# One transformer block on one core: a first tile in plain float32, two fewer dot products on TensorE, and a rewritten tail

## The chip, the core and the metric

The kernel runs on one core of one Trainium2 chip. The time is the device time of one execution in microseconds (us); lower is better. Before the change it is 1208.03 us, the median of three runs (1205.26 to 1211.31 us). The execution that was profiled took 1210.78 us, of which the profile's span covers 1209.1 us. Time zero in every table is the span's start.

## The reference

What is computed is one block over 512 tokens of width 1024, all in float32, with feature-major activations (a tile holds 128 features of all 512 tokens):

```python
mod = einsum('bd,de->be', silu(c), w_ada) + b_ada
shift1, scale1, gate1, shift2, scale2, gate2 = split(mod, 6)
hmix = modulate(rmsnorm(x, g_norm1), shift1, scale1)      # h*(1+scale)+shift
proj = einsum('bsd,de->bse', hmix, w_in)                  # 16 stick-breaking heads, 4 retention heads, gates
...
x = x + gate1 * einsum(merged, w_out)
hffn = modulate(rmsnorm(x, g_norm2), shift2, scale2)
a, u = split(einsum(hffn, w_ffn_in), 2)
x = x + gate2 * einsum(silu(a) * u, w_ffn_out)
return rmsnorm(x, g_final)
```

Three places matter here. The **opening** makes shift1 and scale1 (each of their 1024 values is a dot product of a column of w_ada with silu(c)), the modulated rmsnorm, and the projections of the first retention head. The **last product** is the one with w_ffn_out, and the **tail** adds it to the residual, takes the mean of squares over the features for each token, and writes the scaled result.

## The kernel before

TensorE multiplies float32r operands. To keep float32 accuracy nearly every matrix product is made of three: each operand is split into a high part (a copy rounded to float32r, made by ScalarE) and a low part (the remainder, made by VectorE), and the three products high*high, low*high and high*low are summed in PSUM.

**The opening** (lines 435 to 546) is written in a fixed order for TensorE, VectorE and ScalarE (`manual_schedule`): each engine runs its instructions as the program lists them. The eight steps kt = 0 to 7 go over the eight feature tiles. Step kt multiplies the modulated tile `hs[kt]` with 768 weight columns: 256 each of the first retention head's q, k and v. `qk_products` makes the q and k part (four products of 512 columns, or eight of 256), `v_products` the v part (four of 256). For each tile n the other engines prepare:

- `dot(n, half)` on VectorE (line 384): the dot products for the shift (half 0) or the gain (half 1), a 128x1024 multiplication with accumulation. `PE_SHIFT` lists the tiles whose shift is made by TensorE instead, by `dot_pe(n)` (line 393): eight float32 products with one column. Before, the list is 0, 1 and 4.
- `mod_shift` and `mod_gain` on ScalarE (lines 400, 405): the two 128x1 columns.
- `h_t` on VectorE (line 422): x times gain times the row scale, into `ts[n]`; `h_hi` on ScalarE (line 428): adds the shift and rounds to the high part; `h_lo` on VectorE (line 431): the low part.
- `w_hi` on ScalarE (line 411) and `w_lo` on VectorE (line 415): the parts of the weights.

The rows of w_ada and the weights come by DMA, issued in order by SP, into 8 buffers (`sraw`, two per tile) and 3 buffers (`raw`, one per step). `keep_busy(n)` (line 453) issues n products whose result nobody reads.

**Between** the opening and the last product the instructions are ordered by the framework's scheduler, not by hand. The remaining dot products with w_ada (line 254, on VectorE, fed by DMA into two buffers called `araw`) are spread through this part by it, up to about 180 us.

**The tail** (lines 1327 to 1374) is ordered by hand again. Eight output tiles d each get a product (`gemm`), a residual (VectorE, line 924: x1 = product*gate + x1), squares (ScalarE, line 1345), and a sum of squares over tiles (VectorE, line 1201, `add_square`). Tiles 0 to 2 are done whole; tiles 3 to 7 (`LAST`) in token halves h0 (0 to 255) and h1 (256 to 511). A product with a matrix of ones sums over the partitions (`mm(s0, ones, ...)`, in float32); `rsqrt_rows` (lines 320 to 324: two ScalarE and three VectorE instructions) makes the row scale; `final_norm` (line 1133, VectorE) scales a tile's half and sends it to memory, on ScalarE's queue for odd tiles of h1 and on SP's for the rest.

Of the kernel before, what the change touches and what calls it, by code (L numbers as in the profile page):

```python
# [14 lines left out]
AF = mybir.ActivationFunctionType  # L15
# [19 lines left out]
C_RQ, C_RK, C_RV, C_RG, C_BR = 3072, 4096, 5120, 7168, 9216  # L35


PE_SHIFT = (0, 1, 4)


FF_CHUNKS = ((0, 1), (1, 2), (3, 2), (5, 2), (7, 2), (9, 2))
# [72 lines left out]
def kernel(  # L114
# [44 lines left out]
    def f(ap):  # L159
        return ap.bitcast(F32)  # L160
# [274 lines left out]
    with tc.manual_schedule(engines={nc.vector.engine, nc.scalar.engine, nc.tensor.engine}):  # L435

        nc.scalar.preload_act_table_set("natural_log_exp_and_others")
        c = sm[:, SM_C : SM_C + KT]
        nc.scalar.activation(ccol, c, AF.Exp, scale=-1.0)
        nc.vector.tensor_scalar(ccol, ccol, 1.0, None, op0=ALU.add)  # L440
        nc.vector.reciprocal(ccol, ccol)
        nc.vector.tensor_mul(ccol, ccol, c)
        cb = [psz(), psz()]
        for k in range(KT):
            mm(cb[k // 4][:, (k % 4) * P : (k % 4 + 1) * P], ccol[:, k : k + 1].to_broadcast([P, P]),
               ident, k % 4 == 0, k % 4 == 3)
# [6 lines left out]
        def keep_busy(n):  # L453


            for _ in range(n):
                mm(busy, negones, negones[:, 0:1].to_broadcast([P, S]), True, True)

        keep_busy(6)

        sq = {}
        for j in range(KT):
            sq[j] = tmp()
            if j == 3:
                nc.vector.tensor_mul(sq[j], xts[j], xts[j])
            else:
                nc.scalar.activation(sq[j], xts[j], AF.Square)
            if j == 4:
                nc.vector.tensor_copy(cact[:, 0:S], cb[0])
            elif j == 6:  # L470
                nc.scalar.activation(cact[:, S:], cb[1], AF.Copy)
            if 0 < j < 6:
                nc.vector.tensor_add(sq[0], sq[0], sq[j])
# [24 lines left out]
        def qk_products(w, act, hv, start=False, stop=False):  # L498
            for i in range(4):
                mm(qk_ps[i][:, hv], w[:, i * P : (i + 1) * P], act[:, hv], start, stop)  # L500

        def v_products(act, w, blocks, start=False, stop=False):
            for b in blocks:
                o = v_ps[b // 2][:, (b % 2) * 256 : (b % 2) * 256 + 256]
                mm(o, act[:, b * P : (b + 1) * P], w[:, 512:768],
                   start and b % 2 == 0, stop and b % 2 == 1)

        for kt in range(KT):
            if kt == 3:
                nc.vector.tensor_copy(negtri, con[:, P : 2 * P])  # L510
            nx = kt + 1
            if nx + 1 < KT:
                raws[nx + 1] = ada_load(nx + 1)
                wts[nx + 1] = start_weight(nx + 1)
            if nx < KT and nx not in PE_SHIFT:
                dot(nx, 0)
            h_lo(kt)
            _, hi, lo = wts[kt]
            ah, al = hs[kt][:, 0, :], hs[kt][:, 1, :]
            z = kt == KT - 1  # L520
            if kt == 0:
                for n, hv in enumerate(HALVES):
                    qk_products(hi, ah, hv, n == 0)
                    v_products(ah, hi, (2 * n, 2 * n + 1), True)
                if 1 in PE_SHIFT:
                    dot_pe(1)
                qk_products(lo, ah, ALL)
                v_products(ah, lo, range(4))
            else:
                qk_products(hi, ah, ALL)  # L530
                qk_products(lo, ah, ALL)
                if nx + 1 in PE_SHIFT:
                    dot_pe(nx + 1)
                v_products(ah, hi, range(4))
                v_products(ah, lo, range(4))
            qk_products(hi, al, ALL, False, z)
            v_products(al, hi, range(4), False, z)
            if nx < KT:
                dot(nx, 1)
                mod_shift(nx)  # L540
                mod_gain(nx)
                w_lo(nx)
                h_t(nx)
                h_hi(nx)
            if nx + 1 < KT:
                w_hi(nx + 1)
# [789 lines left out]
    with tc.manual_schedule(engines={nc.vector.engine, nc.scalar.engine, nc.tensor.engine}):  # L1336
        banks = {d: ps() if d < 7 else psa() for d in LAST}

        def out_half(d, hv):
            gemm(banks[d][:, hv], wts[d], acts, t0=hv.start, t1=hv.stop)  # L1340

        def out_square(d, hv):
            residual(d, banks[d], 40, hv)
            sq = tmp()[:, 0:256]
            nc.scalar.activation(sq, x1[d][:, hv], AF.Square)  # L1345
            return sq

        for d in LAST:
# [3 lines left out]
        r = tmp()  # L1352
        out_half(3, h1)
        mm(s0, ones, acc[:, h0], True, True)
        rsqrt_rows(s0, r[:, h0])
        add_square(out_square(3, h1), h1)
        for d in LAST[1:4]:
            out_half(d, h1)
        for d in LAST[1:3]:
            add_square(out_square(d, h1), h1)  # L1360
        for d in range(3):
            final_norm(d, h0, r[:, h0])
        add_square(out_square(6, h1), h1)
        out_half(7, h1)
        mm(s1, ones, acc[:, h1], True, False)
        for d in range(3, 5):
            final_norm(d, h0, r[:, h0])
        sq = out_square(7, h1)
        mm(s1, ones, sq, False, True)
        for d in range(5, 8):  # L1370
            final_norm(d, h0, r[:, h0])
# [68 lines left out]
```

## Time and profile before

| what | number |
|---|---|
| median of three runs | 1208.03 us (1205.26 to 1211.31) |
| profiled execution | 1210.78 us, span 1209.1 us |
| TensorE busy (products) | 1182.2 us, 98% of the span |
| VectorE busy | 830.5 us, 69% |
| ScalarE busy | 555.0 us, 46% |
| opening, to the end of step kt = 7 | up to 58.46 us |
| tail, from the first half product to the end | 1178.95 to 1209.1 us |

PE stands for TensorE's products and PEld for its loads of the stationary operand, DVE for VectorE, ACT for ScalarE, POOL for GpSimd and SPq for the DMA issues of SyncE. A row of the timeline has the start, the busy time, the engine, the line, the operation, the tiles (written <- read), the shapes, the number of instructions merged into the row, and in brackets how long the engine sat idle before it and whom it waited for. L226 is the helper through which every product goes, so products are told apart by their tiles. A row of the windows has the busy time of each engine in the stretch, the clock that TensorE was granted (1.00 is full) and the DMA engines' share. A float32 product shows as two records, a float32r product as one.

### The profile page before, as it was taken

How to read it: one execution, taken by the hardware profiler on the slowest of the kernel's cores; microseconds unless marked ns; L12 is line 12 of the kernel's file. 1: busy time of each engine (PE TensorE's matmuls, PEld its weight loads, DVE VectorE, ACT ScalarE, POOL GpSimd, SP SyncE). 2: the span in 40 equal slices, each digit the busy share in tenths (PEclk: the TensorE clock that was granted, in tenths of full speed). 3: DMA queues.
4: the chain of work that ended last, by engine and by line, in shares of the span. 5: the costliest groups of instructions: out<-in, count | busy, mean ns of one | idle time of the engine just before them, and what ended most of it. 6: DMA issues, size and time to landing. Idle time of an engine off the chain costs nothing.

```text
span 1209.1 us, 17051 instructions
## 1 busy us (share of the span) xinstructions
PE 1182.2 (98%) x6739; PEld 1038.7 (86%) x6739; DVE 830.5 (69%) x1274; ACT 555.0 (46%) x823; POOL 31.4 (3%) x60
## 2 busy tenths in 40 slices
PE   8999999999999999999999999999999999999995
PEld 7887777888888888898989888889999999999985
DVE  6888886545555534377878888756988776677656
ACT  5443223332332322377677777345844444454332
POOL 0010000000000000000000000000100000000000
PEclk8999999999999999999999999999999999999998
DMA  9746772231243155535353635643446653565322
GB/s 358 247 131 226 233 252 71 87 105 53 87 122 87 55 149 147 147 92 126 101 136 97 161 82 160 232 122 96 100 137 174 184 161 106 149 185 142 104 71 70
DMA packets 53136, 167.72 MB, mean 139 GB/s; under 512 B 6592, under 2 KB 8768, under 8 KB 53056
## 3 DMA queue, kind: packets, MB, share of 16 engines
q1 hardware_dynamic: 49168, 154.04, 41.6%
q0 software_dynamic: 3312, 12.06, 5.4%
q8 instruction: 53, 0.87, 0.3%
q10 hardware_dynamic: 576, 0.52, 0.1%
q14 instruction: 27, 0.22, 0.1%
HBM read 135.67 MB, written 4.19 MB: 116 GB/s over the span
## 4 chain that ended last, share of the span: by engine, by line
PE 85%; DVE 6%; DMA 4%; ACT 2%; issue 2%; POOL 0%; SPq 0%; DVEq 0%; POOLq 0%; ACTq 0%
PE ps L226 61%; PE z L226 21%; DMA araw<-wada 3%; PE av L226 3%; DVE araw L254 1%; DVE o L1133 0%; DMA o<-xT 0%; DMA h<-h 0%; DVE o L924 0%; ACT h L1208 0%; DVE wlo L207 0%; DVE t L1201 0%; ACT t L1345 0%; DMA t<-t 0%; ACT t L625 0%
## 5 line engine op out<-in xcount | busy, mean ns | idle before, releaser
L226 PE MATMUL ps<-h,whi 128*128 128x512 f32 (+1 forms) x1419 | 418.8, 377 | 0.1
L226 PEld LDWEIGHTS ps<-h,whi 128*128 128x128 f32 x1419 | 258.3, 189 | 44.7 <-ACT h L428 0.7
L205 ACT ACTIVATE whi<-raw 128x1024 fp32r<-128x1024 f32 (+1 forms) x138 | 144.3, 1046 | 283.3 <-PE ps L226 248.4
L226 PE MATMUL ps<-h,wlo 128*128 128x512 f32 (+1 forms) x708 | 264.4, 377 | 0.0
L207 DVE TENSOR_TENSOR wlo<-raw,whi 128x1024 fp32r<-128x1024 f32 (+1 forms) x138 | 166.3, 1206 | 93.5 <-ACT whi L205 56.5
L226 PEld LDWEIGHTS ps<-h,wlo 128*128 128x128 f32 x708 | 133.6, 189 | 23.3
L226 PE MATMUL ps<-s,whi 128*128 128x512 f32 x480 | 149.3, 392 | 1.9 <-DVE v L207 1.9
L226 PE MATMUL ps<-whi,h 128*128 128x256 f32 (+1 forms) x480 | 115.0, 326 | 1.5 <-DVE t L679 1.5
L226 PE MATMUL z<-q,whi 128*128 128x256 f32 x504 | 108.6, 285 | 0.0
L226 PEld LDWEIGHTS ps<-s,whi 128*128 128x128 f32 x480 | 90.1, 190 | 20.5 <-DVE v L207 2.4
L226 PE MATMUL ps<-s,wlo 128*128 128x512 f32 x240 | 94.1, 392 | 0.0
L207 DVE TENSOR_TENSOR s<-t,s 128x512 fp32r<-128x512 f32 (+1 forms) x122 | 77.0, 651 | 24.0 <-ACT s L205 23.7
L226 PEld LDWEIGHTS ps<-whi,h 128*128 128x128 f32 x480 | 82.4, 190 | 10.1 <-DVE t L679 2.3
L205 ACT ACTIVATE s<-t 128x512 fp32r<-128x512 f32 (+1 forms) x122 | 70.8, 598 | 38.4 <-DVE t L789 22.8
L226 PEld LDWEIGHTS z<-q,whi 128*128 128x128 f32 x504 | 86.3, 194 | 1.5
L226 PE MATMUL ps<-wlo,h 128*128 128x256 f32 (+1 forms) x240 | 78.1, 325 | 0.0
L924 DVE SCALAR_TENSOR_TENSOR o<-ps,mod,o 128x512 f32<-128x512 f32 (+1 forms) x63 | 42.4, 680 | 34.7 <-PE ps L226 34.6
L226 PEld LDWEIGHTS ps<-s,wlo 128*128 128x128 f32 x240 | 45.4, 189 | 9.7
L226 PEld LDWEIGHTS ps<-wlo,h 128*128 128x128 f32 x240 | 45.6, 190 | 4.0
L226 PE MATMUL ps<-q,whi 128*128 128x256 f32 (+1 forms) x224 | 48.9, 313 | 0.0
L226 PE MATMUL z<-qp,whi 128*128 128x256 f32 x168 | 47.3, 283 | 0.9 <-DVE t L1314 0.9
L226 PE MATMUL z<-q,wlo 128*128 128x256 f32 x168 | 47.9, 285 | 0.0
(259 smaller groups left out, 1843.2 us busy)
## 6 DMA issues: line engine op xcount, KB each, us to landing
raw<-wp SPq DMA_DIRECT2D x163, 512.0 KB, 3.7
araw<-wada SPq DMA_DIRECT2D x32, 512.0 KB, 4.4
araw<-wp SPq DMA_DIRECT2D x22, 512.0 KB, 5.0
sraw<-wada SPq DMA_DIRECT2D x16, 512.0 KB, 7.8
q<-qp SPq DMA_DIRECT2D x32, 256.0 KB, 3.7
o<-xT SPq DMA_DIRECT2D x16, 256.0 KB, 4.0
q<-qp SPq DMA_DIRECT2D x32, 128.0 KB, 3.3
s<-raw POOLq DMA_DIRECT2D x8, 512.0 KB, 7.4
```

What stands on the lines that cost most here:

```text
L205: nc.scalar.activation(dst_hi, src, AF.Copy, scale=scale)
L207: (eng or nc.vector).tensor_sub(dst_lo, src, f(dst_hi))
L226: nc.tensor.matmul(o, lhs, rhs, start=start, stop=stop, skip_group_check=True)
L254: nc.vector.scalar_tensor_tensor(raw, raw, 1.0, cact, op0=ALU.mult, op1=ALU.mult, accum_out=col)
L924: nc.vector.scalar_tensor_tensor(x1[d][:, hv], o[:, hv], mod[:, gcol + d : gcol + d + 1], x1[d][:, hv], op0=ALU.mult, op1=ALU.add,)
```

## The change

In the opening, `PE_SHIFT` becomes (0,): the shifts of tiles 1 and 4 are made by VectorE. Step kt = 0 no longer works with parts: ScalarE adds the shift in place to `ts[0]`, and TensorE multiplies the float32 tile with the float32 weights as loaded. The high part of `hs[0]`, which later stages read, is made at step 5 and the low part at step 7. In the tail, the order of residuals, squares, additions and scalings is written anew, one sum over the partitions is moved between the products of tile 4, four products of `keep_busy` are put before the last sum, and tile 7's first half is scaled last.

```diff
-PE_SHIFT = (0, 1, 4)
+PE_SHIFT = (0,)
@@ opening
         h_t(0, HALVES[1])
-        w_hi(0)
         mod_shift(0)
         for hv in HALVES:
-            h_hi(0, hv)
-        w_lo(0)
+            nc.scalar.activation(ts[0][:, hv], ts[0][:, hv], AF.Identity, bias=mods[0, 0])
+        hs.append(pair("h"))
         w_hi(1)
...
-            h_lo(kt)
-            _, hi, lo = wts[kt]
+            if kt:
+                h_lo(kt)
+            raw, hi, lo = wts[kt]
...
             if kt == 0:
                 for n, hv in enumerate(HALVES):
-                    qk_products(hi, ah, hv, n == 0)
-                    v_products(ah, hi, (2 * n, 2 * n + 1), True)
-                if 1 in PE_SHIFT:
-                    dot_pe(1)
-                qk_products(lo, ah, ALL)
-                v_products(ah, lo, range(4))
+                    qk_products(raw, ts[0], hv, n == 0)
+                    v_products(ts[0], raw, (2 * n, 2 * n + 1), True)
             else:
...
-            qk_products(hi, al, ALL, False, z)
-            v_products(al, hi, range(4), False, z)
+                qk_products(hi, al, ALL, False, z)
+                v_products(al, hi, range(4), False, z)
+            if kt == 5:
+                nc.scalar.activation(hs[0][:, 0, :], ts[0], AF.Copy)
+            elif z:
+                nc.vector.tensor_sub(hs[0][:, 1, :], ts[0], f(hs[0][:, 0, :]))
@@ tail
         for d in LAST:
             out_half(d, h0)
-            add_square(out_square(d, h0), h0)
+            residual(d, banks[d], 40, h0)
+            if d > 3:
+                add_square(sqs[d - 1], h0)
+            sqs[d] = out_sq(d, h0)
+        add_square(sqs[7], h0)
...
+        out_half(4, h1, range(2))
         mm(s0, ones, acc[:, h0], True, True)
+        out_half(4, h1, range(2, 4))
...
         out_half(7, h1)
+        add_square(sqs[6], h1)
+        residual(7, banks[7], 40, h1)
+        sqs[7] = out_sq(7, h1)
         mm(s1, ones, acc[:, h1], True, False)
-        for d in range(3, 5):
-            final_norm(d, h0, r[:, h0])
-        sq = out_square(7, h1)
-        mm(s1, ones, sq, False, True)
-        for d in range(5, 8):
-            final_norm(d, h0, r[:, h0])
+        keep_busy(4, ps())
+        mm(s1, ones, sqs[7], False, True)
+        norm(h0, range(2, 7))
         rsqrt_rows(s1, r[:, h1])
-        for d in range(8):
-            final_norm(d, h1, r[:, h1])
+        norm(h1, range(8))
+        norm(h0, range(7, 8))
```

How this moves VectorE's instructions at the start of the opening (line 384 is a dot product, 415 the low weights, 422 `h_t`, 431 `h_lo`; the number behind a name is its buffer). Before:

```order
L422 SCALAR_TENSOR_TENSOR t_194<-o_73,sm_192,t_173 128x256
L415 TENSOR_TENSOR wlo_106<-raw_103,whi_105 128x768
L431 SCALAR_TENSOR_TENSOR h_206<-t_194,sm_204,h_206 128x512
L384 SCALAR_TENSOR_TENSOR sraw_109,sm_263<-sraw_109,cact 128x1024
L415 TENSOR_TENSOR wlo_114<-raw_111,whi_113 128x768
L422 SCALAR_TENSOR_TENSOR t_270<-o_75,sm_267,t_173 128x512
```

Behind the low weights and the low part of the first tile stood one dot product of tile 1. With the change, the same stretch of VectorE:

```order
L422 SCALAR_TENSOR_TENSOR t_194<-o_73,sm_192,t_173 128x256
L384 SCALAR_TENSOR_TENSOR sraw_107,sm_223<-sraw_107,cact 128x1024
L384 SCALAR_TENSOR_TENSOR sraw_109,sm_237<-sraw_109,cact 128x1024
L415 TENSOR_TENSOR wlo_114<-raw_111,whi_113 128x768
L422 SCALAR_TENSOR_TENSOR t_244<-o_75,sm_241,t_173 128x512
```

Both parts of the first tile are gone, and two dot products of tile 1 stand there.

VectorE in the tail's second half, behind the row scale of h0 (line 324; line 925 is now the residual, 1202 the addition of squares, 1134 the final scaling; av is the PSUM tile of output tile 7), with the change:

```order
L324 SCALAR_TENSOR_TENSOR t_10819<-t_10931 128x256
L925 SCALAR_TENSOR_TENSOR o_6937<-ps_10815,mod,o_6937 128x256
L925 SCALAR_TENSOR_TENSOR o_6939<-ps_10816,mod,o_6939 128x256
L1202 TENSOR_TENSOR t_10776<-t_10776,t_10938 128x256
L1134 SCALAR_TENSOR_TENSOR o_6929<-o_6929,sm,t_10819 128x256
L1202 TENSOR_TENSOR t_10776<-t_10776,t_10953 128x256
L925 SCALAR_TENSOR_TENSOR o_6941<-ps_10817,mod,o_6941 128x256
L1134 SCALAR_TENSOR_TENSOR o_6931<-o_6931,sm,t_10819 128x256
L1202 TENSOR_TENSOR t_10776<-t_10776,t_10972 128x256
L925 SCALAR_TENSOR_TENSOR o_6943<-av_10818,mod,o_6943 128x256
L1134 SCALAR_TENSOR_TENSOR o_6933<-o_6933,sm,t_10819 128x256
```

Between the row scale of h0 and the residual of tile 7 now stand two scalings; before, five stood there.

More of the change, by code (lines that the diff above doesn't have):

```diff
@@ L451, with keep_busy @@
         busy = ps()
-        def keep_busy(n):
+        def keep_busy(n, busy=busy):
             for _ in range(n):
@@ L1337, with out_half, out_sq @@
         banks = {d: ps() if d < 7 else psa() for d in LAST}
[L1339 to L1343, printed above, removed]
+        def out_half(d, hv, ks=None):
+            gemm(banks[d][:, hv], wts[d], acts, t0=hv.start, t1=hv.stop, ks=ks)
+        def out_sq(d, hv):
             sq = tmp()[:, 0:256]
@@ L1346, in out_square, with norm @@
             return sq
+        r = tmp()
+        def norm(hv, ds):
+            for d in ds:
+                final_norm(d, hv, r[:, hv])
+        sqs = {}
         for d in LAST:
             out_half(d, h0)
-            add_square(out_square(d, h0), h0)
+            residual(d, banks[d], 40, h0)
[3 more added lines that the diff above has]
+        add_square(sqs[7], h0)
         s0, s1 = psz()[:, 0:256], psz()[:, 0:256]
-        r = tmp()
         out_half(3, h1)
+        residual(3, banks[3], 40, h1)
+        sqs[3] = out_sq(3, h1)
+        out_half(4, h1, range(2))
         mm(s0, ones, acc[:, h0], True, True)
+        out_half(4, h1, range(2, 4))
+        add_square(sqs[3], h1)
         rsqrt_rows(s0, r[:, h0])
[L1356 to L1361, printed above, removed]
-            final_norm(d, h0, r[:, h0])
-        add_square(out_square(6, h1), h1)
+        residual(4, banks[4], 40, h1)
+        sqs[4] = out_sq(4, h1)
+        out_half(5, h1)
+        residual(5, banks[5], 40, h1)
+        sqs[5] = out_sq(5, h1)
+        add_square(sqs[4], h1)
+        norm(h0, range(1))
+        out_half(6, h1)
+        add_square(sqs[5], h1)
+        residual(6, banks[6], 40, h1)
+        sqs[6] = out_sq(6, h1)
+        norm(h0, range(1, 2))
         out_half(7, h1)
+        add_square(sqs[6], h1)
+        residual(7, banks[7], 40, h1)
+        sqs[7] = out_sq(7, h1)
         mm(s1, ones, acc[:, h1], True, False)
-        for d in range(3, 5):
-            final_norm(d, h0, r[:, h0])
-        sq = out_square(7, h1)
-        mm(s1, ones, sq, False, True)
-        for d in range(5, 8):
-            final_norm(d, h0, r[:, h0])
+        keep_busy(4, ps())
+        mm(s1, ones, sqs[7], False, True)
+        norm(h0, range(2, 7))
         rsqrt_rows(s1, r[:, h1])
-        for d in range(8):
-            final_norm(d, h1, r[:, h1])
+        norm(h1, range(8))
+        norm(h0, range(7, 8))
 def host_constants():
```

## The prediction

> **What bounds the kernel now.** I read the page first (busy shares, then the chain that ended last), then windows of the stretches that the change touches, then timelines of those stretches.
>
> ```profile
> PE 1182.2 (98%) x6739; PEld 1038.7 (86%) x6739; DVE 830.5 (69%) x1274; ACT 555.0 (46%) x823; POOL 31.4 (3%) x60
> PE 85%; DVE 6%; DMA 4%; ACT 2%; issue 2%; POOL 0%; SPq 0%; DVEq 0%; POOLq 0%; ACTq 0%
> ```
>
> TensorE is busy throughout and carries 85% of the chain: a microsecond saved on TensorE, or in a stretch where TensorE has nothing left to do, is a microsecond of the whole, if nothing between gives it back. The windows show the stretches, and three slices of half a microsecond:
>
> ```profile
> 26.50:58.46 31.96, 31.96 (x192) 28.27 (x191) 28.23 (x45) 13.40 (x25) 0.00 (x0) 1.00 0.75 259
> 84.00:184.00 100.00, 94.24 (x420) 77.10 (x419) 86.11 (x174) 30.91 (x39) 1.03 (x4) 0.98 0.73 232
> 1194.30:1209.10 14.80, 2.44 (x4) 1.00 (x4) 9.34 (x23) 2.12 (x5) 0.00 (x0) 0.60 0.43 142
> 16.00:16.50 0.50, 0.43 (x2) 0.43 (x3) 0.47 (x2) 0.02 (x1) 0.00 (x0) 0.76 1.08 424
> 26.00:26.50 0.50, 0.50 (x2) 0.40 (x2) 0.50 (x1) 0.00 (x0) 0.00 (x0) 0.50 1.01 395
> 26.50:27.00 0.50, 0.50 (x5) 0.46 (x5) 0.50 (x3) 0.29 (x1) 0.00 (x0) 1.00 1.06 416
> ```
>
> After the columns for the engines stand the granted clock and the DMA share. From about 16.25 to 26.5 us, just where the first tile is multiplied, TensorE has half its clock. In the last 14.8 us it is busy for only 2.44: there the end is set by VectorE and ScalarE.
>
> **The opening, TensorE's side.** These rows of TensorE's timeline carry it:
>
> ```profile
> 10.65 2.86 PE L226 MATMUL z<-t,ones 128*128 128x256 f32 x12 [0.91 <-DVE t L473]
> 15.04 0.90 PE L226 MATMUL ps<-negones 128*128 128x512 f32 x3
> 16.07 0.87 PE L226 MATMUL ps<-h,whi 128*128 128x256 f32 x3
> 18.95 3.41 PE L226 MATMUL ps<-mod,sraw 128*128 128x1 f32 x16
> 22.22 1.63 PE L226 MATMUL ps<-h,wlo 128*128 128x512 f32 x3
> 27.06 0.86 PE L226 MATMUL ps<-h,whi 128*128 128x512 f32 x3
> 33.10 1.84 PE L226 MATMUL ps<-mod,sraw 128*128 128x1 f32 x16
> 41.44 0.87 PE L226 MATMUL ps<-h,whi 128*128 128x512 f32 x3
> 45.64 0.87 PE L226 MATMUL ps<-h,whi 128*128 128x512 f32 x3
> 58.46 0.28 PE L226 MATMUL ps<-wlo,h 128*128 128x256 f32 x1
> ```
>
> Step kt = 0 runs from 16.07 to about 26.9, where step 1's first products stand. A later step is 4.2 us (41.44 to 45.64). Step 7 ends by 58.46, and the two thin dot products of `dot_pe` cost 3.41 us at half clock and 1.84 us at full.
>
> The removed work of step 0 is 28 products; the added work is twelve float32 products of 256 columns. The first row prices those: twelve records, six products, 2.86 us, so 0.477 us each at full clock, and by doubling 0.95 at half: 5.7 or 11.4 us for the step. At equal clock they are dearer than the parts (a later step of parts is 4.2 us, against 5.7), so the edit gains only through the clock and through what it takes away.
>
> They can't start earlier: the in-place addition of the shift waits, as the high part did, for the shift of tile 0 from TensorE, at 15.22 on ScalarE:
>
> ```profile
> 15.22 0.26 ACT L400 ACTIVATE sm<-ps,sm 128x1 f32<-128x1 f32 x1
> 15.51 0.51 ACT L428 ACTIVATE h<-t,sm 128x256 fp32r<-128x256 f32 x1
> ```
>
> So the start stays at 16.07, and the drop of the clock at 16.25, which follows work that is not changed, stays too (the last rival asks otherwise). What changes is how soon the clock returns. Before, it returned at 26.5, 4.3 us after the dense products began again at 22.22; the 2.9 us of products from 16.07 to 18.95, followed by 3.4 us of thin one-column products, had not brought it back. Now nothing thin follows: the twelve products are dense from 16.07, so by that row the clock returns at 16.07 + 4.3 = 20.4. Then 4.3/0.95 = 4.6 products are done and 7.4 remain, 3.5 us: step 0 ends at 23.9. Bounds: no drop at all gives 21.8, no return before 26.5 gives 27.0.
>
> The Trainium skill ("TensorE: Matmul & The Clock Gate", Part 1) says that the clock is half or full and is set from free-running windows of about 3.4 us, one busy window being enough. The trace agrees in the distance: 16.25 to 26.5 is three such windows. By that rule the clock is back at 19.7 and step 0 ends about 0.3 us sooner, which would move the result by as much.
>
> Steps 1 to 7 are then 7 x 4.2 = 29.4 us, without the second thin product: the end is 53.3 instead of 58.46, **5.2 us earlier**.
>
> **Does VectorE keep up?** It takes over two dot products and loses two parts:
>
> ```profile
> 16.43 0.48 DVE L422 SCALAR_TENSOR_TENSOR t<-o,sm,t 128x256 f32<-128x256 f32 x1
> 16.83 0.95 DVE L415 TENSOR_TENSOR wlo<-raw,whi 128x768 fp32r<-128x768 f32 x1
> 22.97 0.75 DVE L422 SCALAR_TENSOR_TENSOR t<-o,sm,t 128x512 f32<-128x512 f32 x1 [2.51 <-ACT sm L405]
> 37.98 0.74 DVE L431 SCALAR_TENSOR_TENSOR h<-t,sm,h 128x512 fp32r<-128x512 f32 x1
> 42.46 0.75 DVE L431 SCALAR_TENSOR_TENSOR h<-t,sm,h 128x512 fp32r<-128x512 f32 x1
> L384 DVE SCALAR_TENSOR_TENSOR sraw<-sraw,cact 128x1024 f32<-128x1024 f32 x13 | 15.8, 1218 | 0.9 <-DMA sraw<-wada 0.9
> ```
>
> A dot product is 1.22 us. Before, VectorE then stood 2.51 us waiting for the shift of tile 1, which came from TensorE's slow thin products; that wait goes. From 16.9 now: two dot products 2.4, low weights 0.9, `h_t` 0.7, so `h_t(1)` ends at 20.9 instead of 23.7. From there a full step of VectorE is 4.48 us (37.98 to 42.46), and with the dot product of tile 4 restored every step is a full one: `h_t(7)` at 20.9 + 6 x 4.48 + 0.2 (a cast in step 3) = 48.0, ScalarE's part done by 48.8, and step 7 ends at 53.0 at the earliest. TensorE's 53.3 is just later. Had the clock not dropped, VectorE would be the bound, at 53.0: no better than 5.5 us of gain. The two parts of `hs[0]` moved to steps 5 and 7 (0.6 us of ScalarE, 0.7 of VectorE) lie beside TensorE's 4.2 us of a step; uncovered, the second would cost 0.7.
>
> **The DMA behind it.** The float32 weights are read by TensorE until step 0 ends, so the buffer of the first `raw` tile comes free at about 23.9 instead of 17.8, and SP, in order, holds the weights of tile 3 and all that stands behind them:
>
> ```profile
> 17.80 0.33 SPq L200 DMA_DIRECT2D raw<-wp  x1
> raw<-wp SPq DMA_DIRECT2D x8, 384.0 KB, 7.4
> raw<-wp SPq DMA_DIRECT2D x5, 512.0 KB, 3.7
> ```
>
> SP can issue nothing in the meantime, so what stands before it on the DMA engines drains, and I take the 3.7 us of the quieter loads: landed at 27.6, parts made by about 29.4, while VectorE wants to make that low part at 28.3 and TensorE needs step 3 at 32.3. It is covered by 2 us or so. With the 7.4 us of the crowded loads it lands at 31.3, `h_t(3)` slips to 33.9 and step 3 starts about 2.3 us late: a rival below.
>
> **The tail.** Its rows, engine by engine:
>
> ```profile
> 1187.85 0.70 PE L226 MATMUL z<-t,ones 128*128 128x256 f32 x2
> 1194.02 0.28 PE L226 MATMUL av<-h,wlo 128*128 128x256 f32 x1
> 1199.39 1.22 PE L226 MATMUL z<-t,ones 128*128 128x256 f32 x2 [0.47 <-ACT t L1345]
> 1190.82 0.42 DVE L324 SCALAR_TENSOR_TENSOR t<-t 128x256 f32<-128x256 f32 x1
> 1198.35 0.48 DVE L924 SCALAR_TENSOR_TENSOR o<-av,mod,o 128x256 f32<-128x256 f32 x1
> 1202.98 3.26 DVE L1133 SCALAR_TENSOR_TENSOR o<-o,sm,t 128x256 f32<-128x256 f32 x8
> 1188.94 0.47 ACT L320 ACTIVATE t<-z,eps 128x256 f32<-128x256 f32 x1 [1.60 <-PE z L226]
> 1200.65 0.47 ACT L320 ACTIVATE t<-z,eps 128x256 f32<-128x256 f32 x1 [1.31 <-PE z L226]
> ```
>
> Tile 7's product is there at 1194.3, but its residual starts at 1198.35, four microseconds late: VectorE, in order, stands behind scalings of h0. A product of 256 columns is 0.12 us at full clock and one of 512 is 0.23 (a step's 4.2 us are twelve of each). In the new order, the sum s0 moves behind six more products (0.72 us; it then no longer starts with the last addition at 1187.85 but at 1188.3), so the scale of h0 is done at 1191.7 instead of 1191.24. Eight scalings in a row take 3.26 us, 0.41 each; I price a residual alike and an addition, which is shorter, at 0.35. Behind the scale of h0 VectorE has four residuals, three additions and two scalings up to the end of tile 7's residual: 3.5 us, 1195.2. Its squares, one ScalarE instruction of this size, are ready at 1195.65. On TensorE the first sum of h1 starts after the third addition, 1194.75, takes 0.48, and four products of `keep_busy` follow at 0.23 each, so the last sum starts at 1196.15 instead of 1199.39, and, at full clock instead of half, ends sooner: ScalarE's logarithm starts 1.09 us after (as for s0: 1187.85 to 1188.94), 1197.25, against 1200.65. From there the chain is the same, but nine scalings end it, not eight: 3.4 - 0.4 = **3.0 us earlier**. Bounds: with the clock dropped meanwhile `keep_busy` costs 1.8 us and the gain is 1.5; with the ninth scaling hidden behind the last transfers it is 3.4.
>
> **Sum.** 5.2 + 3.0 = 8.2 us, against the profiled execution: 1210.78 becomes 1202.6. That execution is 2.75 us above the median; from the median, 1199.8. I take 1201.0, between them, since part of the spread of the runs may be the clock drop itself (last rival), which the change mostly removes.
>
> **Between the two places** lies the part that the scheduler orders, and it orders anew what comes between about 70 and 200 us. These are the chain by lines from 69 to 200 us one row of its waits, and the loads' time to landing:
>
> ```profile
> by line: DMA araw<-wada 30.2%; PE ps L226 14.4%; DVE araw L254 13.7%; PE z L226 12.9%; issue 5.6%; DVE wlo L207 2.6%; PE av L226 2.3%; DVE t L681 2.0%; ACT whi L205 1.7%; DVE q L207 1.4%; DVE s L209 1.4%; DVE t L680 1.4%; ACT s L205 1.3%; D
> DVE araw L254 <- DMA araw<-wada: 9.7, 13, 1.0
> araw<-wada SPq DMA_DIRECT2D x32, 512.0 KB, 4.4
> ```
>
> A transfer into one of two buffers and a dot product on VectorE, in turn, are 44% of this chain. The chain starts behind the first head's attention, so it should start 5 us earlier with everything else; that is why I let the gain pass. TensorE is idle there for 5.8 us (window 84 to 184) all the same.
>
> **Rivals.**
> *Late clock*: the float32 products don't count as dense, and full clock returns at 26.5. Step 0 ends at 27.0, step 7 at 56.4; gain 2.1 + 3.0 = 5.1: 1204.1 (sum like above, 3.1 us worse). Against it: the six float32 products at 10.65 ran at full clock.
> *Held transfers*: 7.4 us to land; gain 5.9: 1203.3. For it: the DMA share of 1.01 to 1.08; against: the backlog drains.
> *Swallowed*: the araw chain has a start of its own, which doesn't move; the opening's 5.2 us are waited away, and the tail's 3.0 remain: 1206.2.
> *Slower*: the new order puts dot products ahead of weight splits (line 207) on VectorE, in places where the transfer has only been issued; TensorE then has no weights for a transfer and a dot product, 4.4 + 1.2 us. One such place leaves 2.6 us of the gain; from the second (11.2 us) the change is slower, and three give 1217.8. For it: the same two instructions are 44% of the chain already; against: of the 13 waits for such a transfer none was over 1.0 us.
> *Clock phase*: in some runs the clock doesn't drop at 16 us. Before, step 0 would then be 4.2 + 1.84 us, ending at 22.1: 4.8 us less, 1206.0, which is inside the three runs. The changed kernel is VectorE's 53.0 either way, so it stays at 1202.3.
>
> **How the numbers follow.** Forecast 0.48, late clock 0.10, held transfers 0.12, swallowed 0.18, slower 0.06, clock phase 0.06. A difference under 0.5% (6.0 us: 1202.0 to 1214.1) is about what a measurement can't tell from none. The forecast lies on the fast side of 1202.0 in nine cases of ten, held transfers and clock phase in four of ten, late clock in two: faster 0.52, same 0.42, slower 0.06. The range takes in the bounds and most of the swallowed case: 1196.5 to 1207; the forecast's own is 1198 to 1204.
>
> **What would show it.** Right: step 1's first products at 23 to 24.5, granted clock 1.00 from about 20.5, the end of step 7 near 53.3, the last sum near 13 us before the end, tile 7's residual within 1 us of its product. Wrong: clock at 0.50 to 26.5; ScalarE waiting for tile 3's `raw` at 27 to 31; the end of step 7 early but the same stages at 200 us unmoved; TensorE idle over 10 us between 84 and 184.

## The result, and the profile after

The changed kernel takes **1203.65 us**, the median of 21 runs (1200.64 to 1208.30); the kernel before, in 21 runs beside them, 1210.94 us (1205.07 to 1216.07). The ratio is **0.995**, 95% interval 0.9934 to 0.9965: 0.5% less time, with an interval that leaves out 1. A second comparison, on another occasion, gave 0.9941 (0.992 to 0.9962). The profiled execution took 1201.79 us (span 1200.0), 9.0 us less than the profiled execution of before. That is more than the medians' difference of 7.3 and the ratio's 6.0 (0.5% of 1210.94); the surplus over the medians is where the two profiled executions lie among their own runs, 1.9 us below the median for the changed kernel (1201.79 against 1203.65) and 0.2 below it for the kernel before. What differs between executions of one kernel is the main thing that the experiments had to settle.

The page of the changed kernel, busy shares and chain by engine:

```profile
PE 1173.0 (98%) x6707; PEld 1030.7 (86%) x6707; DVE 831.2 (69%) x1277; ACT 554.6 (46%) x823; POOL 32.4 (3%) x60
PE 86%; DVE 6%; DMA 4%; ACT 2%; issue 2%; POOL 0%; SPq 0%; DVEq 0%; POOLq 0%; ACTq 0%
```

TensorE is busy 9.2 us less in a span that is 9.1 us shorter: it is still what the end waits for. The windows of the changed kernel (behind the engines' busy time the granted clock, the DMA share and GB/s):

```profile
16.77:23.55 6.78, 6.78 (x24) 5.68 (x25) 6.75 (x12) 3.46 (x7) 0.00 (x0) 0.75 1.02 381
17.00:17.50 0.50, 0.50 (x3) 0.39 (x3) 0.47 (x2) 0.00 (x0) 0.00 (x0) 0.65 1.09 434
20.50:21.00 0.50, 0.50 (x4) 0.45 (x3) 0.50 (x2) 0.00 (x0) 0.00 (x0) 0.94 1.01 401
23.55:53.59 30.04, 30.04 (x172) 26.24 (x171) 30.04 (x47) 13.83 (x26) 0.00 (x0) 1.00 0.87 316
79.00:179.00 100.00, 94.80 (x423) 77.57 (x421) 86.58 (x174) 30.48 (x39) 0.60 (x2) 0.98 0.74 233
```

The clock still drops, at 17.15 us (the half microsecond from 17.00 has a mean of 0.65), but it is back at 20.5, after one stretch of 3.4 us instead of three. From 23.55 to 53.59 TensorE and VectorE are both busy for the whole 30.04 us. TensorE's timeline in the opening:

```profile
11.34 2.86 PE L226 MATMUL z<-t,ones 128*128 128x256 f32 x12 [2.85 <-DVE t L473]
16.77 2.60 PE L226 MATMUL ps<-t,raw 128*128 128x256 f32 x6
23.55 1.04 PE L226 MATMUL ps<-h,whi 128*128 128x512 f32 x3
44.80 0.95 PE L226 MATMUL ps<-h,whi 128*128 128x512 f32 x3
49.31 0.94 PE L226 MATMUL ps<-h,whi 128*128 128x512 f32 x3
53.59 0.28 PE L226 MATMUL ps<-wlo,h 128*128 128x256 f32 x1
```

The whole start is 0.7 us later in this execution (the column sums at 11.34 instead of 10.65). Step 0 begins at 16.77, step 1 at 23.55, step 7 ends at 53.6. Counted from the start of step 0, that is 36.82 us where it was 42.39 (16.07 to 58.46). Steps 6 and 7 begin 4.51 us apart (44.80, 49.31). Before, they were 4.44 apart, since two products of 256 columns stand between them (54.04 and 54.16 before, 49.08 and 49.20 now). TensorE's timeline of before:

```profile
49.84 0.87 PE L226 MATMUL ps<-h,whi 128*128 128x512 f32 x3
54.04 0.28 PE L226 MATMUL ps<-whi,h 128*128 128x256 f32 x1
54.28 0.86 PE L226 MATMUL ps<-h,whi 128*128 128x512 f32 x3
```

The 30.04 us of steps 1 to 7 are thus 7 x 4.2, the 0.24 us of these two products, and 0.4 us more, most of it in rows with which a step starts (1.04, 0.95 and 0.94 us against 0.87). Step 7 starts at 49.31 because ScalarE's high part of tile 7 is done only then, and that waits for VectorE. In VectorE's timeline nothing is idle (no brackets): its low weights for steps 5, 6 and 7 start 4.49 and 4.48 us apart. ScalarE's row, then VectorE's:

```profile
48.51 0.73 ACT L428 ACTIVATE h<-t,sm 128x512 fp32r<-128x512 f32 x1 [1.14 <-DVE t L422]
...
37.89 0.96 DVE L415 TENSOR_TENSOR wlo<-raw,whi 128x768 fp32r<-128x768 f32 x1
42.38 0.95 DVE L415 TENSOR_TENSOR wlo<-raw,whi 128x768 fp32r<-128x768 f32 x1
46.86 0.95 DVE L415 TENSOR_TENSOR wlo<-raw,whi 128x768 fp32r<-128x768 f32 x1
```

The tail, from TensorE's, VectorE's and ScalarE's timelines:

```profile
1188.13 0.28 PE L226 MATMUL av<-h,wlo 128*128 128x256 f32 x1
1190.57 0.59 PE L226 MATMUL z<-t,ones 128*128 128x256 f32 x2
...
1175.07 0.48 DVE L925 SCALAR_TENSOR_TENSOR o<-ps,mod,o 128x256 f32<-128x256 f32 x1 [0.68 <-PE ps L226]
1189.03 0.48 DVE L925 SCALAR_TENSOR_TENSOR o<-av,mod,o 128x256 f32<-128x256 f32 x1
1193.54 3.65 DVE L1134 SCALAR_TENSOR_TENSOR o<-o,sm,t 128x256 f32<-128x256 f32 x9
...
1183.48 0.47 ACT L320 ACTIVATE t<-z,eps 128x256 f32<-128x256 f32 x1 [0.21 <-PE z L226]
1189.54 0.42 ACT L1345 ACTIVATE t<-o 128x256 f32<-128x256 f32 x1 [0.89 <-DVE o L925]
1191.20 0.47 ACT L320 ACTIVATE t<-z,eps 128x256 f32<-128x256 f32 x1 [1.25 <-PE z L226]
```

Tile 7's last product ends at 1188.4 (1188.13 + 0.28) and its residual starts at 1189.03, 0.6 us behind it instead of four. From the first half residual of tile 3 (1175.07; 1180.59 before) to the span's end are 24.93 us; before 28.51.

Where the profiles' 9.1 us come from, by these marks (the fourth ends with the second head's first instruction on GpSimd, at 182.97 and 178.40):

| stretch | before | after | difference |
|---|---|---|---|
| start to step 0 | 16.07 | 16.77 | +0.70 |
| step 0 to the end of step 7 | 42.39 | 36.82 | -5.57 |
| to the second head's GpSimd work | 124.51 | 124.81 | +0.30 |
| to the tail's first half residual | 997.62 | 996.67 | -0.95 |
| tail | 28.51 | 24.93 | -3.58 |

The fourth row holds a drop of the clock at 876 to 880 us in the execution of before (1.7 us) that the changed kernel's doesn't have; but for it that stretch would be 0.8 us longer, and the middle as a whole (third and fourth rows) would give back about 1 us.

### The profile page after: what moved, and what is told of

It reads as the page before. It is cut to its first block, busy times and chain, and to the rows that moved or that the text cites. A ratio compares the mean times of both kernels' runs of the same rounds, so it can differ in the third digit from the quotient of the medians.

```text
span 1200.0 us, 16991 instructions
## 1 busy us (share of the span) xinstructions
PE 1173.0 (98%) x6707; PEld 1030.7 (86%) x6707; DVE 831.2 (69%) x1277; ACT 554.6 (46%) x823; POOL 32.4 (3%) x60
## 4 chain that ended last, share of the span: by engine, by line
PE 86%; DVE 6%; DMA 4%; ACT 2%; issue 2%; POOL 0%; SPq 0%; DVEq 0%; POOLq 0%; ACTq 0%
PE ps L226 62%; PE z L226 21%; PE av L226 3%; DMA araw<-wada 3%; DVE araw L254 1%; DVE wlo L207 1%; DMA h<-h 0%; DMA o<-xT 0%; ACT h L1209 0%; DMA t<-t 0%; DVE o L1134 0%; ACT t L626 0%; DVE t L473 0%; DVE s L209 0%; DVE t L682 0%
## 5 line engine op out<-in xcount | busy, mean ns | idle before, releaser
L925 DVE SCALAR_TENSOR_TENSOR o<-ps,mod,o 128x512 f32<-128x512 f32 (+1 forms) x63 | 42.4, 681 | 35.5 <-PE ps L226 35.5
```

The source lines that it names most:

```text
L925: nc.vector.scalar_tensor_tensor(x1[d][:, hv], o[:, hv], mod[:, gcol + d : gcol + d + 1], x1[d][:, hv], op0=ALU.mult, op1=ALU.add,)
```

## The experiments

**Theory**: the opening's gain is the clock's early return plus VectorE work taken away, the tail's is VectorE freed for tile 7's residual, and both pass through the middle undiminished. **Rivals**: the opening's gain depends on the execution (whether the clock drops in step 0 at all), and it is the removed thin products and not the float32 tile that earn it.

### Each half alone, and the change again

`opening_only` has the new opening and the old tail, `tail_only` the reverse:

```diff
 opening_only: PE_SHIFT = (0,), float32 step 0, parts of hs[0] at steps 5 and 7; tail as before
 tail_only:    PE_SHIFT = (0, 1, 4), step 0 in parts; tail as changed
```

> The new opening with the old tail. Theory (the gain of each place is kept to the end): step 7 ends near 53.5 us as in the changed kernel, against 58.5 before; the tail from the residual of tile 3's first half to the end stays at 28.5 us; the whole is about 5 us faster, ratio 0.996. Rival (the opening's gain is waited away in the middle): step 7 as early, but the whole is at most 2 us faster, ratio above 0.998.

> The old opening with the new tail. Theory: everything up to the tail is as before (step 7 ends at 58.5 us), the tail from the residual of tile 3's first half to the end takes 25.0 us, not 28.5, ratio 0.997. Rival (the tail only looked shorter because the changed kernel met another phase of the clock): the tail takes 27 us or more, ratio 0.999 or above.

> The changed kernel once more, beside the three below. Both theories: 5 to 7 us under the kernel before, ratio 0.995.

| kernel | ratio (95%) | step 0 to end of step 7 | tail |
|---|---|---|---|
| opening_only | 0.9981 (0.9963 to 0.9998) | 36.82 us | 28.19 us |
| tail_only | 0.9977 (0.9955 to 0.9999) | 42.22 us | 24.97 us |
| after_again | 0.9941 (0.992 to 0.9962) | 36.82 us | 24.99 us |

Each half shortens its own stretch by the same amount alone as together, and leaves the other's as it was within 0.3 us: the two add up. (In `tail_only`, whose opening is that of the kernel before, the clock was at half for three stretches in a row again, from 18.7 to 28.9 us.) The tail alone should give 3.5/1210 = 0.29%, and gives 0.23% within its interval. The opening alone shortens its stretch by 5.57 us, 0.46%, and gives only 0.19%, with 0.37% as the interval's end: its gain in the profile is more than its gain over many executions.

TensorE's timeline of `opening_only`:

```profile
16.05 1.56 PE L226 MATMUL ps<-t,raw 128*128 128x256 f32 x6
21.51 0.96 PE L226 MATMUL ps<-h,whi 128*128 128x512 f32 x3
52.87 0.28 PE L226 MATMUL ps<-wlo,h 128*128 128x256 f32 x1
```

Here the clock didn't drop: six records take 1.56 us, not 2.60, and step 0 takes 5.46 us instead of 6.78. Step 7 still ends 36.82 us after the start of step 0. The dropped clock costs the new opening nothing; VectorE sets its length.

### The thin products or the float32 tile?

`shifts_only` is the kernel before with one edit, `shifts_back` the changed kernel with that edit undone:

```diff
 shifts_only (the kernel before)
-PE_SHIFT = (0, 1, 4)
+PE_SHIFT = (0,)
 shifts_back (the changed kernel)
-PE_SHIFT = (0,)
+PE_SHIFT = (0, 1, 4)
...
                     v_products(ts[0], raw, (2 * n, 2 * n + 1), True)
+                dot_pe(1)
```

> The kernel before with only the list changed: the shifts of tiles 1 and 4 on the vector engine, the first tile still in parts, the old tail. Theory (the thin one-column products carried the cost, by their own time and by keeping the clock low): step 0 is dense, the clock returns about 20.4 us, step 0 ends at 22.5 to 23; the vector engine, which still makes both parts of the first tile (1.5 us more than in the changed kernel), is then the bound and step 7 ends near 55, 3.5 to 4 us earlier than before; ratio 0.997. Rival (the float32 first tile makes the gain): step 7 ends at 57 or later.

> The changed kernel with the shifts of tiles 1 and 4 given back to thin one-column products, the first of them behind step 0; first tile in float32, new tail. Theory: step 0 ends near 23.8 us, the thin product and what waits for the shift of tile 1 put step 1 at about 26.5, the second thin product costs 1.8 us more, step 7 ends at 57 to 58: of the opening's gain under 1.5 us is left, and the whole is about 4 us faster than before (ratio 0.9965), the tail's part. Rival (float32 makes the gain): step 7 ends at 55.5 or earlier, ratio 0.994.

`shifts_only`: ratio 0.9967 (0.995 to 0.9985), median 1205.23 us. `shifts_back`: 1.0002 (0.9983 to 1.002), 1210.88 us, although it has the new tail. TensorE's timeline, first of `shifts_only`:

```profile
16.24 0.62 PE L226 MATMUL ps<-h,whi 128*128 128x256 f32 x3
23.24 0.96 PE L226 MATMUL ps<-h,whi 128*128 128x512 f32 x3 [1.78 <-ACT h L428]
54.59 0.28 PE L226 MATMUL ps<-wlo,h 128*128 128x256 f32 x1
```

and of `shifts_back`:

```profile
19.13 1.56 PE L226 MATMUL ps<-t,raw 128*128 128x256 f32 x6
24.41 1.84 PE L226 MATMUL ps<-mod,sraw 128*128 128x1 f32 x16
28.43 0.96 PE L226 MATMUL ps<-h,whi 128*128 128x512 f32 x3 [2.17 <-ACT h L428]
61.46 0.28 PE L226 MATMUL ps<-wlo,h 128*128 128x256 f32 x1
```

Without the thin products but with parts, the stretch is 38.35 us (16.24 to 54.59); TensorE is done early and waits 1.78 us for the high part of tile 1, which waits for VectorE. The float32 tile takes another 1.53 us off (36.82): that is the time of the two parts that VectorE no longer makes (16.83 to 18.36 us in the profile of before), not anything on TensorE. With the thin products kept, the float32 tile brings nothing: 42.33 us (19.13 to 61.46), with step 1 waiting 2.17 us for a shift that comes from TensorE behind the whole of step 0. So in this stretch the float32 tile pays only beside the removed thin products. As a whole `shifts_back` gains nothing, where about 4 us were expected: against an execution of before without a drop its opening loses (below), and its stretch from step 7 to the second head took 126.14 us, 1.6 more than before, with one drop in each. How the rest divides wasn't separated.

`shifts_only` has a further gain that is not the opening's: the stretch behind it, to the second head's GpSimd work, took 121.33 us instead of 124.51. Of those 3.2 us, 1.7 are a clock drop that its execution doesn't have (before: at 156 to 160 us); the other 1.5 go with the order that the scheduler lays anew. With the float32 tile that stretch changes the other way: without a drop in it, it takes 122.92 us in a second profile of the kernel before (`before_look1`, next part), 123.84 in `after_again` and 124.16 in `opening_only`. So what the float32 tile gains over `shifts_only` in the opening, 1.53 us, is lost again by the second head (2.5 to 2.8 us), and as a whole kernel the one-line edit (0.9967) isn't behind `opening_only` (0.9981). Which instructions of the new order cost this isn't shown, and the one-line edit wasn't run with the new tail.

### The kernel before, three more times

The profiled execution of before had the clock at half from 16.25 to 26.5, but `opening_only` and `shifts_only` ran their openings without a drop. So the unchanged kernel was profiled again.

> The kernel before, unchanged, profiled again. Theory (the drop of the clock in step 0 depends on where an execution's windows fall, and costs the kernel before several us): from the start of step 0 to the end of step 7 it takes 42.4 us where the granted clock is at half for the whole of step 0, 39 to 41 where it is at half for one or two windows of 3.4 us, and 37.5 to 38.5 where it doesn't drop. Rival (the stretch is set by something other than the clock, such as VectorE's wait for a shift): 42 to 42.5 whatever the clock shows.

> As the run above: 42.4 us from the start of step 0 to the end of step 7 with the clock at half throughout step 0, 39 to 41 with one or two windows at half, 37.5 to 38.5 with none; by the rival 42 to 42.5 in each case.

> As the two runs above: 42.4 us with the clock at half throughout step 0, 39 to 41 with one or two windows at half, 37.5 to 38.5 with none; by the rival 42 to 42.5 in each case.

TensorE's timeline of `before_look1`:

```profile
16.46 0.61 PE L226 MATMUL ps<-h,whi 128*128 128x256 f32 x3
18.71 1.84 PE L226 MATMUL ps<-mod,sraw 128*128 128x1 f32 x16
23.30 0.86 PE L226 MATMUL ps<-h,whi 128*128 128x512 f32 x3
54.71 0.28 PE L226 MATMUL ps<-wlo,h 128*128 128x256 f32 x1
```

and step 0 in the windows, of `before_look1` and then of `before_look3`:

```profile
16.46:23.30 6.84, 6.37 (x45) 5.82 (x46) 6.49 (x11) 3.14 (x6) 0.00 (x0) 1.00 1.04 410
```

```profile
16.73:27.79 11.06, 11.01 (x45) 9.95 (x45) 8.51 (x14) 3.81 (x8) 0.00 (x0) 0.54 1.03 408
```

| execution of before | clock in step 0 | step 0 | step 0 to end of step 7 | time |
|---|---|---|---|---|
| the first profile | half | 10.99 us | 42.39 us | 1210.78 us |
| `before_look1` | full | 6.84 us | 38.25 us | 1207.29 us |
| `before_look2` | full | 6.38 us | 37.80 us | 1209.70 us |
| `before_look3` | half | 11.06 us | 42.47 us | 1212.06 us |

In these four executions the same program does the opening in 38 or in 42.4 us, with nothing between: a drop that falls into step 0 lasts three stretches of 3.4 us. (That it slows the thin products, 1.84 to 3.41 us, and so prolongs what keeps the clock down, fits, but wasn't tried.) `tail_only` (42.22 us) makes it three drops in five executions of this opening. `before_look2` had a drop of one stretch ahead of step 0 instead (granted clock 0.50 from 12 to 14 us): its step 0 starts at 17.86, 1.4 us later than in `before_look1`, which a count from step 0 leaves out. This is what the profile of before alone couldn't show. The changed opening takes 36.82 us either way. So its gain is 5.6 us in an execution of before that drops and 1.0 to 1.4 us in one that doesn't, where the stretch behind it gives back some 0.9 (123.84 against 122.92 us); and the same holds of the parts: against the 38.0 us without a drop, `shifts_only` (38.35) gains nothing, and `shifts_back` (42.33, of which 1.7 are a drop at 29 to 33 us) loses some 2.6.

The Trainium skill ("TensorE: Matmul & The Clock Gate", Part 1) says that the clock's window of about 3.4 us is free-running and doesn't start with the kernel, so that the same kernel meets it at another point in each run. The four executions agree. The page puts the penalty of the clock's ramp under 1% of a typical kernel's span, and here too it is less: 4.4 of 1209 us, 0.4%. That is still nearly as much as the whole change.

### Dense products between the thin ones

The one remaining set of thin products (tile 0's shift) gets four dense products whose result nobody reads:

```diff
             ... eight one-column products of dot_pe(0)
+            if k % 2:
+                mm(busy, negones, negones[:, 0:1].to_broadcast([P, S]), True, True)
```

> The changed kernel with four more dense products whose result nobody reads, one behind every second thin product of tile 0's shift, so that the clock should not drop at 16 to 17 us. Theory (the vector engine bounds the changed opening): the clock is 1.00 from 13 to 27 us, step 0 starts up to 1 us later and takes 5.7 us instead of 6.8, but step 7 still ends within 0.5 us of the changed kernel's. Rival (the clock still bounds the opening): step 7 ends 1 us or more earlier, by as much as step 0 ends earlier.

The ratio is 0.9944 (0.9919 to 0.9969), median 1202.36 us. There is no drop in step 0, which takes 5.10 us; but it starts at 16.91, behind a longer thin stretch, and step 7 ends at 53.1, where it ends at 53.2 in `after_again`, which had a drop. From the first thin product to the end of step 7 both take 39.56 us (13.53 to 53.09, 13.61 to 53.17). A shorter step 0 buys nothing here, again because VectorE sets the length. Since `opening_only` had no drop either without these products, that they prevent it isn't shown.

### The tail: the fill and the last scaling

`tail_no_busy` leaves out the four products ahead of the last sum. `tail_short` keeps two of them and scales tile 7's first half with the others, ahead of the row scale of h1:

```diff
 tail_no_busy
-        keep_busy(4, ps())
 tail_short
-        keep_busy(4, ps())
+        keep_busy(2, ps())
-        norm(h0, range(2, 7))
+        norm(h0, range(2, 8))
-        norm(h0, range(7, 8))
```

> The changed kernel without the four dense products before the last sum. Theory (they delay the last sum more than they help, since the clock drops only 4 us later): the last sum starts as soon as the squares of tile 7 are there, about 0.5 us sooner, at full clock, and the tail from the residual of tile 3's first half is 24.5 us instead of 24.9. Rival (they hold the clock): without them the last sum runs at half clock, ends 0.5 us later than with them, and the tail takes 25.2 us or more.

> The changed kernel with two of those products instead of four, and tile 7's first half scaled before the row scale of the second half, so that eight scalings end the kernel, not nine. Theory: the last sum starts 0.5 us sooner and one scaling of 0.4 us moves into the vector engine's wait for the row scale: the tail takes 24.1 us, 0.8 less than the changed kernel. Rival (the end is set by the last transfers out, not by the scalings): the tail takes 24.5 us or more.

The tails are 24.51 and 24.23 us against 24.93; the ratios, 0.9946 (0.9925 to 0.9968) and 0.9948 (0.9927 to 0.9969), can't tell half a microsecond. TensorE's and VectorE's timelines of `tail_no_busy`:

```profile
1188.80 1.54 PE L226 MATMUL z<-t,ones 128*128 128x256 f32 x4 [0.77 <-DVE t L1202]
1192.71 3.65 DVE L1134 SCALAR_TENSOR_TENSOR o<-o,sm,t 128x256 f32<-128x256 f32 x9
```

and of `tail_short`:

```profile
1190.44 0.59 PE L226 MATMUL z<-t,ones 128*128 128x256 f32 x2
1193.47 3.26 DVE L1134 SCALAR_TENSOR_TENSOR o<-o,sm,t 128x256 f32<-128x256 f32 x8
```

The four fills cost 0.42 us net: they delay the last sum past the point where its squares are ready (1189.54 + 0.42 = 1189.96 in the changed kernel, where it starts at 1190.57). Nor do they hold the clock for it: without them the clock is at full until 1194.1, behind the last sum. The ninth scaling costs what it takes, 0.39 us (3.65 less 3.26): the last scalings and not the transfers behind them set the end.

### The pieces together

`best` is the changed kernel with the dense products of `dense_thin`, no fill in the tail, and the scaling of `tail_short`:

> The changed kernel with four dense products put between the thin ones of tile 0 (no clock drop in step 0), without the products that fill TensorE ahead of the last sum, and with tile 7's first half scaled along with the others. Theory (the pieces add up): the tail takes 23.8 to 24.2 us instead of 24.93, step 0 to step 7 takes 36.2, the ratio to the kernel before is 0.993 to 0.9945. Rival (the fill kept TensorE's clock up for the last sum, and the scalings are hidden behind transfers): the tail takes 24.9 us or more, ratio 0.995 or above.

Step 0 to the end of step 7 is 36.15 us and the tail 24.15, both as the theory had them, but the ratio is 0.9957 (0.9936 to 0.9979) and the median of eight runs 1203.73 us: no better than the changed kernel, which by the theory's ratio it should have beaten. The windows of `best` show where its profiled execution (1204.04 us) lost time:

```profile
128.00:134.00 6.00, 5.73 (x18) 4.52 (x19) 5.64 (x11) 1.32 (x3) 0.00 (x0) 0.72 0.72 243
180.00:184.00 4.00, 4.00 (x17) 3.71 (x17) 0.69 (x2) 0.35 (x1) 0.54 (x2) 0.59 0.19 71
872.00:878.00 6.00, 4.68 (x26) 4.68 (x27) 2.77 (x5) 0.63 (x1) 0.00 (x0) 0.72 1.01 322
```

Three drops of one window each between the opening and the tail, up to 1.7 us apiece, where the changed kernel's profile had one (150 to 154 us). The 0.67 us from step 0 on (36.82 to 36.15) are no gain of the opening: from the first thin product to the end of step 7 it is 39.54 us, against 39.56, as step 0 only starts later. What is left to expect is the tail's 0.78 us, less than one window of the clock, so eight runs don't show it; whether it is there stays open.

## Why the prediction was right, and where it wasn't

The forecast was 1202.6 us for the profiled execution and 1201.0 for the median; they are 1201.79 and 1203.65. The first is 0.8 us off, although several of the terms behind it were wrong and partly cancelled, which is luck; the second is 2.65 us off, because of the number that the sum started from.

**The clock's return.** The forecast had a drop at 16.25, the clock back at 20.4, 4.3 us behind the start of step 0, and step 0 of 7.8 us (16.07 to 23.9). Measured, the drop came at 17.15 and the return at 20.5, 3.4 us later, which is the shorter of the two distances that the prediction named. Step 0 took 6.78 us (16.77 to 23.55), 1.05 less, also because a float32 product of 256 columns took 0.425 us at full clock (5.10 us for twelve in `dense_thin`), not 0.477. The late clock (full clock only at 26.5) is refuted: float32 products count as dense work. But the step from the clock to the gain fails: `opening_only`, without a drop there, ends step 7 after the same 36.82 us.

**Steps 1 to 7 on TensorE, VectorE "just earlier".** The forecast had TensorE set the end at 53.3 and VectorE at 53.0, which is 37.2 and 36.9 us from the start of step 0. It was the other way round. TensorE alone would have needed 6.78 + 29.4 + 0.24 = 36.4 us, the 0.24 being the two products ahead of step 7 that the forecast left out; VectorE, without a gap at 4.48 us a step, sets 36.82. The gain of 5.2 us was measured as 5.57 from the start of step 0, and 4.87 on the span's own clock, since everything started 0.7 us later. VectorE's sum was right to 0.1 us; TensorE's, which made the forecast, was 0.8 us too long, and the size came out because the two stood 0.3 us apart.

**The weights of tile 3.** The forecast had their buffer held by step 0 until 23.9. SyncE's and ScalarE's timelines (the fourth `raw` issue, the next one, and `w_hi` of tiles 2 and 3):

```profile
20.79 0.33 SPq L200 DMA_DIRECT2D raw<-wp  x1
23.93 0.33 SPq L200 DMA_DIRECT2D raw<-wp  x1
...
22.09 0.83 ACT L411 ACTIVATE whi<-raw 128x768 fp32r<-128x768 f32 x1
26.57 0.83 ACT L411 ACTIVATE whi<-raw 128x768 fp32r<-128x768 f32 x1
```

They were issued at 20.79, before step 0 had ended, so they didn't go into tile 0's buffer; tile 1's low weights had just been made (VectorE, 19.81 + 0.95 us). Tile 4's load is the one that followed step 0, at 23.93. The step was wrong, its result (no wait at 26.57) right, and the rival of held transfers falls with it.

**The tail.** Forecast 3.0 us, measured 3.58 (3.54 in `tail_only`). The last sum came 3.30 us earlier within the tail (18.80 to 15.50 us after tile 3's first half residual), against 3.24 forecast. The mis-sized term is what follows it: ScalarE's logarithm was put 1.09 us behind the start of the last sum, and starts 0.63 behind (1190.57 to 1191.20), as that sum runs at full clock. The 0.4 us for the ninth scaling was right, as `tail_short` shows, so the bound with that scaling hidden is out. The row scale of h0 isn't held up by the sum's new place either: it is done 10.70 us after tile 3's first half residual (1185.35 + 0.42), 10.65 before, where 0.46 later was forecast. One sign was misstated: the last sum was to stand near 13 us before the end, which counts from the end of before; it stands 9.4 us before its own end (9.7 before the change).

**The middle.** The prediction let the gain pass, and most of it passed: +0.30 us and -0.95 us in the two stretches between. But the -0.95 is a clock drop fewer; without it the middle gives back about 1 us, as do the profiles without a drop behind the opening (122.92 to 123.84), and the forecast had nothing for that. The swallowed case is refuted by the second head's start, 4.57 us earlier (182.97 to 178.40), and the slower case by TensorE's 94.80 us of 100 where it had been 94.24. The dot products' new places starve nothing.

**From the profile to the median.** The sum started from 1208.03 us, the median of three runs, and 21 runs of the same kernel have a median of 1210.94: 2.9 us, more than the whole miss. The gain that 1201.0 amounts to, 1208.03 - 1201.0 = 7.0 us, is what the medians show (7.3) and lies at the upper end of the two ratios (0.5% and 0.59%, 6.0 and 7.1 us). Nor did the profiled execution lie 2.75 us above the median; it lies 0.2 below that of the 21 runs.

What failed in the mechanism is the step that the drop at 16.25 "follows work that is not changed, stays too". It stays in some executions only. The rival on the clock's phase priced an opening of before without the drop at 4.8 us less; measured, it is 4.1 to 4.6. What was wrong is the chance: 0.06, where two of four profiles of before have no drop (two of five executions with `tail_only`). The tail's 3.5 us are there in every comparison, the opening's gain is 1.2 us or 5.6, and 0.3 to 0.9 are given back on the way to the second head; at half and half that is an estimate of 3.5 + 3.4 less 0.3 to 0.9, 6.0 to 6.6 us, which the two comparisons bear out.

## What to carry to other kernels

A clock drop seen in one profile is a property of that execution: before an edit is priced by it, profile the kernel before again, and price the edit with the drop and without. Start the sum from more than three runs: here their median was 2.9 us off, and the gain was 7. Thin products on TensorE in a stretch with little else cost most through the clock, and moving them to another engine removes the dear case only as far as that engine isn't the next bound; here VectorE was, within 0.3 us. When a change has several parts, run the smallest one alone as a whole kernel: here the one-line edit showed no smaller gain than the whole new opening (0.33% and 0.19%, with intervals that overlap), and in the profiles what the float32 tile saved went again in the part behind it. In a tail that is ordered by hand, put the residual that the last sum needs ahead of scalings that nobody waits for, and take fills and late scalings out once the sum is no longer late.

## What the runs showed of the hardware that was not expected

Drops of TensorE's granted clock come in whole windows of about 3.4 us, and one costs about half its length where TensorE is the bound: from the first head's GpSimd work to the second's, the kernel before took 109.94 us with one (73.03 to 182.97) and 108.35 without (`before_look1`). The same program gets a different set of them in each execution: before, three in a row in step 0 or none, and in `before_look2` one ahead of it. Over the 21 runs of the changed kernel time and mean granted clock go together (correlation -0.84: at 0.998, 1200.64 us; at 0.995, 1201.19 to 1203.65; at 0.991 to 0.992, 1204.55 to 1208.30), so much of what looked like a spread of the measurement is the number of such windows. Float32 products bring the clock back like any other dense work, after one window (17.15 to 20.5), while each drop in step 0 comes within 3.4 us of eight float32 products with one column, which TensorE's rows show as 1.84 us of uninterrupted work. In `before_look1` and `before_look2` those products were followed by no drop there, so they don't decide it alone.
